# Feature-major projections: both PSUM banks of a block as one tile

## The chip, the cores and the metric

The kernel runs on one core of one Trainium2 chip. The metric is the device time of one execution in microseconds (us), taken as the median of three runs. A core has five engines that run their own instruction streams in order and meet through semaphores: PE (matrix multiply, with PEld, its weight loads), DVE (vector), ACT (scalar), POOL, and SP, which issues most of the DMAs. Matmul results land in PSUM, 128 partitions by 8 banks of 2 KB; everything else that the engines work on lies in SBUF.

## The reference

One layer of an encoder trunk on 256 tokens of width 2048, all in float32. Only the sizes matter here:

```python
h = rms_norm(x, norm_mix_g)
proj = h @ w_in                       # 2048 -> 18464, split in ten parts
rq, rk = rope(...)                    # retention: 8 heads, chunks of 64
q, k, v = silu(causal_conv(gqkv))     # gated delta rule: 16 heads of 128
x = x + (sigmoid(ga) * yr + sigmoid(gb) * yg) @ w_out
q = rms_norm(x) @ w_q ; k, v = split(rms_norm(mem) @ w_kv)
x = x + (softmax(q k^T) v) @ w_o      # 4 heads of 512, 256 memory tokens
x = x + square(relu(rms_norm(x) @ w_ff1)) @ w_ff2    # hidden 8192
return rms_norm(x)
```

## The kernel before, in words

**Products in three parts.** Each float32 operand is split in a rounded high part and the rest (`hi` by an ACT copy, `lo` by a DVE subtraction, lines 125 and 126 for weights). A product is hi·hi + hi·lo + lo·hi. Weights come from HBM in pieces of 1 MB (`raw`, three buffers), and each piece is split in two steps of 128x1024 elements into `whi` and `wlo` (three buffers each; in the last stage every fourth piece uses a single further pair `whx`, `wlx`).

**Feature-major blocks.** `blocks_in_steps` computes 256 output features for 256 tokens: the weights are the stationary operand, the activations the moving one. A block has two groups of 128 features, b = 0 and 1, one PSUM bank each (`s0` and `s1`). Line 210 issues for each of 16 steps of the contraction and each b one matmul of 512 columns (`whi` against hi and lo side by side) and one of 256 columns (`wlo` against hi), so 64 matmuls in a block. At the end, for each b apart, ACT copies the second half of the bank to a tile `bo` (line 219), DVE adds the first half (line 220), and a function of the caller, `evac(b, o)`, goes on with 128x256 elements. There are 96 blocks: 8 for the keys of the memory, 24 for the delta rule's q, k, v, 8 for retention's q, k, 8 in each of two residual projections (`residual_pass`), 8 for the cross-attention's q and 32 for `w_ff1`.

**Token-major products** (`chunk`, lines 166 to 168, and the second MLP product, line 1227 in `with_seven`) use the same PSUM tiles through `stream_ps()`, for tokens 0 to 127 and 128 to 255. In `with_seven` the finished bank is added to the result by line 1142 (`res = bank * r + res`, 128x512 on DVE); `own[n][t]` is the bank of column group n and token half t, `read((n, t, bank))` notes that it is to be added, and the next product puts the addition ahead of its own matmuls.

**What sets the order.** A scheduler places each engine's instructions from the program text, priorities (`tc.high_priority`) and its own forecast of times; `tc.issue_after` fixes some pairs. Then the engines run these fixed orders. A tile of a pool is given out again when its last readers are done: `s0`, `s1` have two buffers each, so a block uses the banks of the block before the last. In three of four parts of the MLP (`early`) the order of blocks and products on PE is fixed by `ends`; in the first part and in the residual passes the scheduler may mix the matmuls of neighbouring blocks.

Beside these, `residual_pass` sums squares in `acc2` and closes with four matmuls of `acc2` against ones (line 1042); `evac_h` makes the squared ReLU of the MLP's hidden layer (lines 1432 to 1438).

Of the kernel before, what the change touches and what calls it, by code (L numbers as in the profile page):

```python
# [17 lines left out]
P = 128  # L18
# [34 lines left out]
def trunk(ctx: ExitStack, tc: tile.TileContext, x_f, mem_f, positions, lead_f, small_f, w_in, ret_gn_g, w_out, w_xq,  # L53
# [12 lines left out]

    def stream_ps():
        s0 = psp.tile([P, 512], F32, name="s0", tag="s0", bufs=2)
        s1 = psp.tile([P, 512], F32, name="s1", tag="s1", bufs=2)
        return s0, s1  # L70
# [121 lines left out]
    def blocks_in_steps(quads, w, c0, nb, evac, ends=None, even=False):  # L192

        k = 16 // nb
        ps = stream_ps()
        n = nb * P
        for g in range(KT // k):  # L200
            halves = fetch([(0, w[g * k * P:(g + 1) * k * P, c0:c0 + n])], k, n, at=AT_BLOCKS)
            for h in range(2):
                these = [(i, b, part) for i in range(k // 2) for b in range(nb) for part in range(2)]
                if even and g == h == 0:
                    these.sort(key=lambda a: a[2])
                for i, b, part in these:
                    kk = (2 * g + h) * k // 2 + i
                    x = quads[kk // 4][0] if part else quads[kk // 4].both
                    with tc.issue_after(ends[-1]) if ends else ExitStack():
                        ins = pe.matmul(ps[b][:, :S] if part else ps[b], halves[h][part][:, i, b * P:(b + 1) * P],  # L210
                                        x[:, kk % 4, :], start=kk == 0 and not part, stop=kk == KT - 1 and part == 1).ins
                if ends is not None:
                    ends.append(ins)
                step()
                yield
        for b in range(nb):
            with tc.high_priority(offset=50000):
                o = sm.tile([P, S], F32, name="bo", tag="bo", bufs=2)
                act.activation(o, ps[b][:, S:], AF.Copy)  # L219
                vec.tensor_add(o, o, ps[b][:, :S])  # L220
                evac(b, o)
# [5 lines left out]
    def narrow(quads, w, c0, n, evac):  # L227
# [12 lines left out]
        with tc.high_priority(offset=50000):  # L240
            o = sm.tile([P, S], F32, name="bo", tag="bo", bufs=2)[:n]
# [382 lines left out]
    for b2 in range(8):  # L624
        ko = kv.tile([P, 2, S], F32, name="ko", tag="vo", bufs=2)

        def evac_k(b, ps):
            vec.tensor_mul(ko[:, b, :], ps, mrow)
# [35 lines left out]
    def gdn_stream(grp):  # L664
# [3 lines left out]
        for pr in range(2):  # L668
# [5 lines left out]
            for part, c0, bofs in ((1, C_GQ, 0), (0, C_GK, 16), (2, C_GV, 32)):  # L674
                def evac(b, ps, part=part, bofs=bofs):
                    if part < 2:
                        conv_silu(bofs + h0 + b, ps, kq[:, b, part, :])
                    else:
                        vt = mx.tile([P, S], F32, name="vt", tag="vt", bufs=2)
                        conv_silu(bofs + h0 + b, ps, vt)  # L680
                        vts.append(vt)
                blocks(h1, w_in[0], c0 + h0 * GD, 2, evac)
# [6 lines left out]
            for b in range(2):  # L689
# [12 lines left out]
                for t, src in enumerate((g0v[:, 0, 0:P], g1v[:, 0, :])):  # L702
                    dj = sm.tile([P, S], F32, name="dj", tag="bo", bufs=2)[:, :P]
# [162 lines left out]
    def retention(j, yr):  # L866
        qk = mx.tile([P, 4, S], F32, name="qk", tag="qk", bufs=1)

        for a2, c0 in ((0, C_RQ), (2, C_RK)):
            def evac_qk(b, ps):  # L870

                rb = mx.tile([P, S], F32, name="rb", tag="rb", bufs=2)
                act.activation(rb[0:64], ps[64:128], AF.Copy)
                act.activation(rb[64:128], ps[0:64], AF.Copy)
                o = qk[:, a2 + b, :]
                vec.tensor_mul(o, ps, cos)
                vec.tensor_mul(rb, rb, sin)
# [131 lines left out]
    def residual_pass(quads, w, gain, name, loader=None, between=None):  # L1009
        nxt = []  # L1010
        acc = xa.tile([P, S], F32, name="acc2", tag="acc2", bufs=2)
        vec.memset(acc, 0.0)
        first_two, held = [], []
        for b2 in range(8):
# [4 lines left out]
            def evac(b, ps, b2=b2, xc=xc):  # L1019
                k = 2 * b2 + b  # L1020
                vec.tensor_add(rt[:, k, :], ps, xc[:, b, :] if loader else rt[:, k, :])
                g = gains[:, gain + k:gain + k + 1]
                qh, ql = (a[:, k % 4, :] for a in nxt[-1])
                act.activation(qh, rt[:, k, :], AF.Copy, scale=g)
                vec.scalar_tensor_tensor(ql, rt[:, k, :], g, qh.bitcast(F32), op0=ALU.mult, op1=ALU.subtract)
                sq = xa.tile([P, S], F32, name="sq2", tag="sq2", bufs=2)
                act.activation(sq, rt[:, k, :], AF.Square)
# [13 lines left out]
        for t in range(NT):  # L1041
            pe.matmul(ps[:, 2 * t:2 * t + 2], acc[:, t * P:(t + 1) * P], ones[:, :2], start=True, stop=True)
# [17 lines left out]
    for h in range(XH):  # L1060
# [10 lines left out]
        for b2 in range(2):  # L1071
            blocks(h2, w_xq[0], h * XD + b2 * 256, 2, lambda b, ps: split(qt, ps, 2 * b2 + b))
# [346 lines left out]
    for fb in range(4):  # L1419
# [5 lines left out]
        for b2 in range(8):  # L1425
# [65 lines left out]
```

## Time and profile before

| what | value |
|---|---|
| three runs | 2044.32, 2045.71, 2046.57 us; median 2045.71 |
| span of the profiled execution, first to last instruction | 2043.3 us |
| PE busy | 2030.5 us (99%), 10802 matmuls |
| PEld busy | 1751.4 us (86%) |
| DVE busy | 1550.6 us (76%) |
| ACT busy | 1184.3 us (58%) |
| the block matmuls of line 210, 512 and 256 columns with `whi`, `wlo` | 969.0 and 765.0 us |
| lines 219 and 220, 192 each | 73.2 and 79.9 us |
| DMA queue q1, share of 16 engines | 62.2% |

Busy time counts an instruction from its start to its end, and matmuls overlap each other. The mean of one 512-column matmul is 390 ns, while the next one starts some 0.23 us after it; the distance of starts is what the stream costs.

### The profile page before, as it was taken

To read this page: it belongs to the slowest core of one execution; us is meant where nothing else is said; L and a number is where in the kernel's file an instruction comes from. 1 tells how busy PE (TensorE), PEld (TensorE's weight loads), DVE (VectorE), ACT (ScalarE), POOL (GpSimd) and SP (SyncE) were. 2 spreads that over 40 slices of the span, in tenths; PEclk is the share of its full clock that TensorE was granted. 3 is DMA by queue.
4 is the path that set the end of the run, shared out by engine and by line. 5 is a ranking of instruction groups with operands and counts; after the bars stand their busy time and mean duration, and the time that the engine had idled before them with its cause. 6 is when DMAs were issued, how large, how long until landed. Compare 5 with 4: busy or idle time off the path is not lost.

```text
span 2043.3 us, 28453 instructions
## 1 busy us (share of the span) xinstructions
PE 2030.5 (99%) x10802; PEld 1751.4 (86%) x10802; DVE 1550.6 (76%) x2423; ACT 1184.3 (58%) x1941; POOL 38.7 (2%) x50
## 2 busy tenths in 40 slices
PE   9999999999999999999999999999999999999998
PEld 7888888988888888888888899888888888888886
DVE  5887788779667875888567666777867887888788
ACT  6655764575457554755446565555547656656655
POOL 0000000000000000000000000000000000000000
PEclk9999999999999999999999999999999999999999
DMA  9689556466555655555467655569657656665761
GB/s 329 209 259 303 184 185 197 154 189 201 180 166 183 198 190 165 186 181 190 156 212 244 191 183 163 174 180 254 221 168 234 219 163 214 201 204 166 242 231 62
DMA packets 329370, 405.24 MB, mean 198 GB/s; under 512 B 34944, under 2 KB 239632, under 8 KB 329104
## 3 DMA queue, kind: packets, MB, share of 16 engines
q1 hardware_dynamic: 328800, 402.74, 62.2%
q8 instruction: 84, 1.38, 0.3%
q10 hardware_dynamic: 432, 0.69, 0.1%
q14 instruction: 54, 0.44, 0.1%
HBM read 389.74 MB, written 11.55 MB: 196 GB/s over the span
## 4 chain that ended last, share of the span: by engine, by line
PE 97%; DVE 2%; issue 0%; DMA 0%; ACT 0%; SPq 0%; DVEq 0%; POOLq 0%; POOL 0%; ACTq 0%
PE s L210 52%; PE s L167 8%; PE s L168 8%; PE s L166 8%; PE b L1227 7%; PE s L1227 7%; PE s L400 1%; PE s L401 1%; PE s L402 1%; PE b L795 1%; PE b L698 1%; PE b L138 1%; PE b L828 1%; PE b L137 1%; PE b L139 1%
## 5 line engine op out<-in xcount | busy, mean ns | idle before, releaser
L210 PE MATMUL s<-q,whi 128*128 128x512 f32 x2816 | 969.0, 390 | 0.6 <-DVE bo L220 0.6
L126 DVE TENSOR_TENSOR wlo<-raw,whi 128x1024 fp32r<-128x1024 f32 x586 | 715.1, 1222 | 296.3 <-ACT whi L125 291.7
L125 ACT ACTIVATE whi<-raw 128x1024 fp32r<-128x1024 f32 x586 | 620.8, 1060 | 488.9 <-PE s L210 209.2
L210 PE MATMUL s<-q,wlo 128*128 128x256 f32 x2816 | 765.0, 281 | 0.0
L210 PEld LDWEIGHTS s<-q,whi 128*128 128x128 f32 x2816 | 520.6, 188 | 101.4 <-DVE bo L220 0.9
L210 PEld LDWEIGHTS s<-q,wlo 128*128 128x128 f32 x2816 | 527.2, 188 | 12.6 <-DVE wlo L126 0.5
L167 PE MATMUL s<-wlo,q 128*128 128x512 f32 x704 | 277.2, 394 | 0.0
L168 PE MATMUL s<-whi,q 128*128 128x512 f32 x704 | 274.9, 391 | 0.0
L166 PE MATMUL s<-whi,q 128*128 128x512 f32 x704 | 254.4, 391 | 0.0
L166 PEld LDWEIGHTS s<-whi,q 128*128 128x128 f32 x704 | 132.1, 188 | 27.4
L168 PEld LDWEIGHTS s<-whi,q 128*128 128x128 f32 x704 | 132.3, 188 | 26.2
L167 PEld LDWEIGHTS s<-wlo,q 128*128 128x128 f32 x704 | 132.3, 188 | 26.2
L219 ACT ACTIVATE bo<-s 128x256 f32<-128x256 f32 x192 | 73.2, 381 | 105.5 <-PE s L210 105.5
L220 DVE TENSOR_TENSOR bo<-bo,s 128x256 f32<-128x256 f32 x192 | 79.9, 416 | 43.0 <-ACT bo L219 42.8
L1227 PE MATMUL s<-whi,q 128*128 128x512 f32 x280 | 90.4, 389 | 0.0
L1250 DVE TENSOR_TENSOR wlo<-rt,whi 128x1024 fp32r<-128x1024 f32 x54 | 65.8, 1224 | 32.3 <-ACT whi L1249 31.6
L210 PE MATMUL s<-q,whx 128*128 128x512 f32 x256 | 89.2, 389 | 0.0
L125 ACT ACTIVATE whx<-raw 128x1024 fp32r<-128x1024 f32 x58 | 61.5, 1060 | 43.2 <-PE b L1227 17.2
L126 DVE TENSOR_TENSOR wlx<-raw,whx 128x1024 fp32r<-128x1024 f32 x58 | 70.9, 1222 | 17.9 <-ACT whx L125 17.4
L1249 ACT ACTIVATE whi<-rt 128x1024 fp32r<-128x1024 f32 x54 | 57.2, 1060 | 38.1 <-PE s L1227 17.8
L210 PE MATMUL s<-q,wlx 128*128 128x256 f32 x256 | 70.4, 280 | 0.0
L1227 PE MATMUL b<-whi,q 128*128 128x512 f32 x216 | 70.3, 389 | 0.0
(350 smaller groups left out, 2372.2 us busy)
## 6 DMA issues: line engine op xcount, KB each, us to landing
raw<-w_in SPq DMA_DIRECT2D x143, 1024.0 KB
raw<-w_ff SPq DMA_DIRECT2D x100, 1024.0 KB
raw<-w_xkv SPq DMA_DIRECT2D x29, 1024.0 KB
raw<-w_out SPq DMA_DIRECT2D x16, 1024.0 KB
raw<-w_xq SPq DMA_DIRECT2D x16, 1024.0 KB
raw<-w_xo SPq DMA_DIRECT2D x16, 1024.0 KB
rt<-w_ff SPq DMA_DIRECT2D x14, 1024.0 KB
tr<-w_ff SPq DMA_DIRECT2D x14, 1024.0 KB
```

Of the source, the lines that this page charges most:

```text
L125: latest["hi"] = act.activation(hi[:, cs], src[:, cs], AF.Copy).ins
L126: latest["lo"] = vec.tensor_sub(lo[:, cs], src[:, cs], hi[:, cs].bitcast(F32)).ins
L137: pe.matmul(o, lhs[0], rhs[0], start=first, stop=False)
L166: pe.matmul(o, xh, wh, start=first, stop=False)
L167: pe.matmul(o, xh, wl, start=False, stop=False)
L168: pe.matmul(o, xl, wh, start=False, stop=last)
L210: ins = pe.matmul(ps[b][:, :S] if part else ps[b], halves[h][part][:, i, b * P:(b + 1) * P], x[:, kk % 4, :], start=kk == 0 and not part, ...
L219: act.activation(o, ps[b][:, S:], AF.Copy)
L220: vec.tensor_add(o, o, ps[b][:, :S])
L1227: ins = pe.matmul(o, lhs[l], rhs[r], start=key not in opened, stop=last and j == 2, skip_group_check=True).ins
L1249: latest["hi"] = act.activation(hi, raw[:, c:c + 1024], AF.Copy).ins
L1250: latest["lo"] = vec.tensor_sub(lo, raw[:, c:c + 1024], hi.bitcast(F32)).ins
```

## The change

Both banks of a block become one PSUM tile `s` of 128x2x512 with two buffers; `stream_ps` hands out its halves. ACT copies 128x2x256 elements with one instruction, DVE adds with one, and each `evac` gets both feature groups at once: 96 copies and 96 additions of 512 elements stand where 192 of 256 stood, and most of what follows (the keys' scaling, the rotation, the residual addition and its squares, the split of q, the squared ReLU) is done for both at once too. The causal convolution and the scaling by the norm's gains stay one instruction for each group. `acc2`, `sq2` and `rb` become 128x2x256 with one buffer instead of two of 128x256; `bo` becomes twice as large with two buffers. `acc2` now holds two groups, so the closing sum has eight matmuls instead of four. The space for `bo` is taken from a reserved area, `dynamic_dma_scratch_size=8192`: in the built programs it goes from 16384 to 8192 bytes of a partition, weights and the tiles behind them move down by 8192 bytes, and the tiles behind `bo` by 6144. No matmul of lines 166 to 168, 210 and 1227 is added, removed or resized.

```diff
+    def stream_both():
+        return psp.tile([P, 2, 512], F32, name="s", tag="s", bufs=2)
+
     def stream_ps():
-        s0 = psp.tile([P, 512], F32, name="s0", tag="s0", bufs=2)
-        s1 = psp.tile([P, 512], F32, name="s1", tag="s1", bufs=2)
-        return s0, s1
+        both = stream_both()
+        return both[:, 0, :], both[:, 1, :]
...
-        ps = stream_ps()
+        both = stream_both()
+        ps = both[:, 0, :], both[:, 1, :]
...
-        for b in range(nb):
-            with tc.high_priority(offset=50000):
-                o = sm.tile([P, S], F32, name="bo", tag="bo", bufs=2)
-                act.activation(o, ps[b][:, S:], AF.Copy)
-                vec.tensor_add(o, o, ps[b][:, :S])
-                evac(b, o)
+        with tc.high_priority(offset=50000):
+            o = sm.tile([P, 2, S], F32, name="bo", tag="bo", bufs=2)
+            act.activation(o, both[:, :, S:], AF.Copy)
+            vec.tensor_add(o, o, both[:, :, :S])
+            evac(o)
...
-            def evac(b, ps, b2=b2, xc=xc):
-                k = 2 * b2 + b
-                vec.tensor_add(rt[:, k, :], ps, xc[:, b, :] if loader else rt[:, k, :])
...
+            def evac(ps, b2=b2, xc=xc):
+                got = rt[:, 2 * b2:2 * b2 + 2, :]
+                vec.tensor_add(got, ps, xc if loader else got)
+                for k in range(2 * b2, 2 * b2 + 2):
...
+                sq = xa.tile([P, 2, S], F32, name="sq2", tag="sq2", bufs=1)
+                act.activation(sq, got, AF.Square)
                 vec.tensor_add(acc, acc, sq)
...
-            pe.matmul(ps[:, 2 * t:2 * t + 2], acc[:, t * P:(t + 1) * P], ones[:, :2], start=True, stop=True)
+            for b in range(2):
+                pe.matmul(ps[:, 2 * t:2 * t + 2], acc[:, b, t * P:(t + 1) * P], ones[:, :2], start=b == 0, stop=b == 1)
...
-            def evac_h(b, ps):
+            def evac_h(ps):
                 if early:
                     act.activation(ps, ps, AF.Relu)
-                    act.activation(hs[:, b, :], ps, AF.Square)
+                    act.activation(hs, ps, AF.Square)
                 else:
-                    vec.scalar_tensor_tensor(hs[:, b, :], ps, 0.0, ps, op0=ALU.max, op1=ALU.mult)
-                qh, ql = (a[:, b2 % 2 * 2 + b, :] for a in hid[-1])
-                act.activation(qh, hs[:, b, :], AF.Copy)
-                vec.tensor_sub(ql, hs[:, b, :], qh.bitcast(F32))
-                if b2 < 4 and b:
+                    vec.scalar_tensor_tensor(hs, ps, 0.0, ps, op0=ALU.max, op1=ALU.mult)
+                split(hid[-1], hs, slice(b2 % 2 * 2, b2 % 2 * 2 + 2))
+                if b2 < 4:
                     token_sums(b2, hs)
...
-    nc = bacc.Bacc("TRN2", target_bir_lowering=False, num_devices=1)
+    nc = bacc.Bacc("TRN2", target_bir_lowering=False, num_devices=1, dynamic_dma_scratch_size=8192)
```

How the orders move is shown at three places. Rows of the change bear the changed kernel's line numbers (213 for 210, 222 for 220, 1232 for 1227, 1147 for 1142); the numbers behind names tell buffers apart, and a bracket names the engines or DMA queues whose semaphores the instruction waits for.

**Place A, PE, the second MLP product, once in each of the three `early` parts:** the end of the product into `own[0][0]` and the start of the one into `own[0][1]`. Before:

```order
L1227 MATMUL s0_15391<-whi_15491,q_14671 128x512 [waits Activation_49]
L1227 MATMUL s0_15391<-wlo_15492,q_14671 128x512 [waits DVE_49]
L1227 MATMUL s0_15391<-whi_15491,q_14671 128x512 x2
L1227 MATMUL s0_15391<-wlo_15492,q_14671 128x512
L1227 MATMUL s0_15391<-whi_15491,q_14671 128x512
L1227 MATMUL s1_15392<-whi_15507,q_14454 128x512 [waits Activation_49]
L1227 MATMUL s1_15392<-wlo_15508,q_14454 128x512 [waits DVE_49]
```

The same place in the change, first on PE and then on DVE:

```order
L1232 MATMUL s_14856<-whi_14954,q_14184 128x512 [waits Activation_49]
L1232 MATMUL s_14856<-wlo_14955,q_14184 128x512 [waits DVE_49]
L1232 MATMUL s_14856<-whi_14954,q_14184 128x512 x2
L1232 MATMUL s_14856<-wlo_14955,q_14184 128x512
L1232 MATMUL s_14856<-whi_14954,q_14184 128x512
L1232 MATMUL s_14856<-whi_14970,q_13983 128x512 [waits DVE_49,Activation_49]
L1232 MATMUL s_14856<-wlo_14971,q_13983 128x512
```

```order
L1255 TENSOR_TENSOR wlo_14971<-rt_9911,whi_14970 128x1024 [waits Activation_49]
L1255 TENSOR_TENSOR wlx_14975<-rt_9911,whx_14974 128x1024 [waits Activation_49]
L128 TENSOR_TENSOR wlo_14994<-raw_14991,whi_14993 128x1024 [waits DMAHW4_49,Activation_49]
L1147 SCALAR_TENSOR_TENSOR res_12593<-s_14856,rstd3q_12587,res_12593 128x512 [waits PE_49]
L128 TENSOR_TENSOR wlo_14998<-raw_14991,whi_14997 128x1024 [waits Activation_49]
```

The two banks are one tile `s_14856` now, and the first matmul into its second bank waits for DVE, where the next matmul, which needs the split `wlo_14971`, waits for nothing more. The DVE count that it waits for is reached by the addition of line 1147 that reads the first bank of the tile. On DVE this addition stands behind the splits of the same product and one split for the next one.

**Place B, PE and DVE, the first residual projection:** `s_9924` is block 0, `s_10022` block 1, `s_10121` block 2, which uses block 0's banks again; before, these are the pairs from `s0_10165`, `s0_10271` and `s0_10378`. PE before, the end of block 0, and 42 rows further on the start of block 2:

```order
L210 MATMUL s1_10166<-q_9832,wlo_10216 128x256
L210 MATMUL s0_10271<-q_10051,whi_10279 128x512 [waits Activation_49]
L210 MATMUL s0_10271<-q_10051,wlo_10280 128x256 [waits DVE_49]
L210 MATMUL s1_10272<-q_10051,whi_10279 128x512
L210 MATMUL s1_10272<-q_10051,wlo_10280 128x256
```

```order
L210 MATMUL s1_10272<-q_9832,whi_10321 128x512
L210 MATMUL s1_10272<-q_9832,wlo_10322 128x256
L210 MATMUL s0_10378<-q_10014,whi_10382 128x512 [waits Activation_49]
L210 MATMUL s1_10379<-q_10014,whi_10382 128x512 [waits DVE_49,PE_49]
L210 MATMUL s0_10378<-q_10014,wlo_10383 128x256 [waits DVE_49]
```

In the change, PE at the end of block 0, PE at the start of block 2, and DVE:

```order
L213 MATMUL s_9924<-q_9593,wlo_9974 128x256
L213 MATMUL s_10022<-q_9847,wlo_10068 128x256
L213 MATMUL s_10022<-q_9593,whi_10071 128x512 [waits Activation_49]
L213 MATMUL s_10022<-q_9593,wlo_10072 128x256 [waits DVE_49]
L213 MATMUL s_10022<-q_9593,whi_10071 128x512
```

```order
L213 MATMUL s_10022<-q_9593,whi_10071 128x512
L213 MATMUL s_10022<-q_9593,wlo_10072 128x256
L213 MATMUL s_10121<-q_9773,whi_10124 128x512 [waits DVE_49]
L213 MATMUL s_10121<-q_9773,wlo_10125 128x256
L213 MATMUL s_10121<-q_9773,whi_10124 128x512
```

```order
L136 TENSOR_TENSOR ktl_10725<-kr_10720,kth_10724 128x1024 [waits DMAHW6_49,Activation_49]
L128 TENSOR_TENSOR wlo_10125<-raw_10122,whi_10124 128x1024 [waits DMAHW2_49,PE_49]
L1075 SCALAR_TENSOR_TENSOR vvl_10727<-vr_10722,nm_r_773,vvh_10726 128x512 [waits DMAHW7_49,Activation_49]
L1075 SCALAR_TENSOR_TENSOR vvl_10727<-vr_10722,nm_r_773,vvh_10726 128x512 [waits Activation_49]
L128 TENSOR_TENSOR wlo_10129<-raw_10122,whi_10128 128x1024 [waits DVE_49,PE_49,Activation_49]
L222 TENSOR_TENSOR bo_10009<-bo_10009,s_9924 128x512 [waits Activation_49]
```

Before, 48 matmuls of block 1 stood between the end of block 0 and the start of block 2; now there are 17. Block 2 waits for the last of these DVE rows, the addition that frees block 0's banks (line 222). The first wait for PE in them, at `wlo_10125`, is for the last matmul of block 0, the first row of the change's PE rows.

**Place C, PE, the start of `w_ff1`:** `s_12604` is block 0, `s_12707` block 1; before, these are `s0_13017` and `s0_13127`, and `s0_13238` is block 2. Before, the end of block 0, and 11 rows further on the first use of `whx` in block 1:

```order
L210 MATMUL s1_13018<-q_12784,whx_13067 128x512
L210 MATMUL s1_13018<-q_12784,wlx_13068 128x256
L210 MATMUL s0_13238<-q_12127,whi_13242 128x512 [waits DVE_49]
L210 MATMUL s0_13238<-q_12127,wlo_13243 128x256
L210 MATMUL s0_13238<-q_12127,whi_13242 128x512
```

```order
L210 MATMUL s0_13238<-q_12366,whi_13246 128x512
L210 MATMUL s0_13238<-q_12366,wlo_13247 128x256
L210 MATMUL s0_13127<-q_12784,whx_13177 128x512 [waits Activation_49]
L210 MATMUL s1_13128<-q_12784,whx_13177 128x512
L210 MATMUL s0_13127<-q_12784,wlx_13178 128x256 [waits DVE_49]
```

In the change:

```order
L213 MATMUL s_12604<-q_12385,whx_12653 128x512
L213 MATMUL s_12604<-q_12385,wlx_12654 128x256
L213 MATMUL s_12707<-q_12385,whx_12756 128x512 [waits Activation_49]
L213 MATMUL s_12707<-q_12385,wlx_12757 128x256 [waits DVE_49]
L213 MATMUL s_12707<-q_12385,whx_12756 128x512
```

`whx` and `wlx` have one buffer each. Between the last use of the old contents of `whx` and the first use of the new ones stood 17 matmuls; now there is one, the 256-column matmul of `wlx_12654`. The wait for DVE ahead of block 2, which stood right behind block 0, now stands 16 matmuls behind it.

More of the change, by code (lines that the diff above doesn't have):

```diff
@@ L674, in gdn_stream, with evac @@
             for part, c0, bofs in ((1, C_GQ, 0), (0, C_GK, 16), (2, C_GV, 32)):
[L675 to L681, printed above, removed]
+                def evac(o, part=part, bofs=bofs):
+                    for b in range(2):
+                        if part < 2:
+                            conv_silu(bofs + h0 + b, o[:, b, :], kq[:, b, part, :])
+                        else:
+                            vt = mx.tile([P, S], F32, name="vt", tag="vt", bufs=2)
+                            conv_silu(bofs + h0 + b, o[:, b, :], vt)
+                            vts.append(vt)
                 blocks(h1, w_in[0], c0 + h0 * GD, 2, evac)
@@ L1010, in residual_pass @@
         nxt = []
-        acc = xa.tile([P, S], F32, name="acc2", tag="acc2", bufs=2)
+        acc = xa.tile([P, 2, S], F32, name="acc2", tag="acc2", bufs=1)
         vec.memset(acc, 0.0)
@@ L1071, in trunk @@
         for b2 in range(2):
-            blocks(h2, w_xq[0], h * XD + b2 * 256, 2, lambda b, ps: split(qt, ps, 2 * b2 + b))
+            blocks(h2, w_xq[0], h * XD + b2 * 256, 2, lambda o: split(qt, o, slice(2 * b2, 2 * b2 + 2)))
         sps = bank()
```

29 lines of the change are left out of this document (14 added, 15 removed).

## The prediction

> **What bounds the kernel now.** I read the first page, then who waited on PE, then the timeline around PE's one long pause. The page's busy shares and chain:
>
> ```profile
> PE 2030.5 (99%) x10802; PEld 1751.4 (86%) x10802; DVE 1550.6 (76%) x2423; ACT 1184.3 (58%) x1941; POOL 38.7 (2%) x50
> PE 97%; DVE 2%; issue 0%; DMA 0%; ACT 0%; SPq 0%; DVEq 0%; POOLq 0%; POOL 0%; ACTq 0%
> ```
>
> PE is busy for all but 13 us, and the chain that ended last runs through it for 97%. A busy PE may still hide waits, so the waits of PE alone, complete:
>
> ```profile
> PE b L258 <- DVE warm L254: 1.1, 1, 1.1
> PE s L400 <- ACT q L348: 0.8, 1, 0.8
> PE s L210 <- DVE bo L220: 0.6, 1, 0.6
> PE s L400 <- DVE q L335: 0.3, 1, 0.3
> ```
>
> Three of the four are start-up. Between start-up and the end only one wait is listed, 0.6 us. So work taken off ACT or DVE has almost nothing to give back, while whatever newly makes PE wait adds its full length: PE has no slack to catch up in. The question is which waits of PE are new.
>
> This is PE's one listed pause at work, in the timeline (start, duration, idle before in brackets), and what it costs:
>
> ```profile
> 1367.93 0.28 PE L210 MATMUL s<-q,wlx 128*128 128x256 f32 x1
> 1368.31 0.42 DVE L220 TENSOR_TENSOR bo<-bo,s 128x256 f32<-128x256 f32 x1 [1.37 <-ACT bo L219]
> 1368.79 0.19 PEld L210 LDWEIGHTS s<-q,whi 128*128 128x128 f32 x1 [0.90 <-DVE bo L220]
> 1368.79 0.50 PE L210 MATMUL s<-q,whi 128*128 128x512 f32 x1 [0.58 <-DVE bo L220]
> 1369.13 0.28 PE L210 MATMUL s<-q,wlo 128*128 128x256 f32 x1
> 1369.24 0.39 PE L210 MATMUL s<-q,whi 128*128 128x512 f32 x1
> 1369.47 0.28 PE L210 MATMUL s<-q,wlo 128*128 128x256 f32 x1
> ```
>
> In the stream a 512-column matmul is followed after 0.23 us (1369.24 to 1369.47), a 256-column one after 0.12 (1369.13 to 1369.24); a pair takes 0.345. Here 0.86 passes after the 256-column one, 0.74 too much. PE goes on 0.06 after DVE's end (1368.31 + 0.42 = 1368.73), and the first distance afterwards is 0.34 instead of 0.23, since the weight load starts only with the matmul: 0.11 more. I use both for every pause. [...]
>
> **The change part by part.**
>
> The larger operations. The rows of what is replaced, and of the nearest operations with 512 elements:
>
> ```profile
> L219 ACT ACTIVATE bo<-s 128x256 f32<-128x256 f32 x192 | 73.2, 381 | 105.5 <-PE s L210 105.5
> L220 DVE TENSOR_TENSOR bo<-bo,s 128x256 f32<-128x256 f32 x192 | 79.9, 416 | 43.0 <-ACT bo L219 42.8
> L133 ACT ACTIVATE q<-b 128x512 fp32r<-128x512 f32 x10 | 5.8, 590 | 6.9 <-PE b L139 5.8 <-PE b L277 1.1
> L693 DVE TENSOR_TENSOR kl<-kq,kh 128x512 fp32r<-128x512 f32 x16 | 11.0, 685 | 0.0
> ```
>
> 96 copies at 0.59 are 56.6 us against 73.2 on ACT, 96 additions at 0.685 are 65.8 against 79.9 on DVE; the later steps save in proportion. All of it lies beside PE and is worth 0 on the path. The cover is the other pair of banks: most blocks (11 us, 32 pairs) have a whole block between their end and the next use of their banks, against 0.59 + 0.69 for the copy and the addition. Where that cover is gone is place B.
>
> Place A, three times. PE may write `own[0][1]` only when DVE has read `own[0][0]`, its neighbour in the tile. Before, these are the rows (1638.14 stands for two matmuls, the second at 1638.37, the first one into `own[0][1]`):
>
> ```profile
> 1638.14 0.62 PE L1227 MATMUL s<-whi,q 128*128 128x512 f32 x2
> 1638.31 1.23 DVE L126 TENSOR_TENSOR wlo<-raw,whi 128x1024 fp32r<-128x1024 f32 x1
> 1639.45 0.74 DVE L1142 SCALAR_TENSOR_TENSOR res<-s,rstd3q,res 128x512 f32<-128x512 f32 x1
> 1808.26 0.62 PE L1227 MATMUL s<-whi,q 128*128 128x512 f32 x2
> 1809.56 0.74 DVE L1142 SCALAR_TENSOR_TENSOR res<-s,rstd3q,res 128x512 f32<-128x512 f32 x1
> 1978.39 0.61 PE L1227 MATMUL s<-whi,q 128*128 128x512 f32 x2
> 1979.69 0.74 DVE L1142 SCALAR_TENSOR_TENSOR res<-s,rstd3q,res 128x512 f32<-128x512 f32 x1
> ```
>
> The addition ends at 1639.45 + 0.74 = 1640.19, PE would go on at 1640.25 instead of 1638.37: 1.88 us. The order on DVE is the same in the change, the split of L126 first. The other two give 1.87 each. With 0.11 each this is 3 x 1.99 = **+6.0**. Were the split out of the way, the addition would start 0.04 after the bank's last matmul, and the pause would still be 0.39 + 0.04 + 0.74 + 0.06 - 0.23 = 1.0: bounds 3.3 to 6.0. Behind PE's wait stands the whole rest of the product; ACT and DVE wait for PE's weights buffers and shift with it.
>
> Place B. DVE rows before at the same place, a pair of splits showing how two in a row overlap:
>
> ```profile
> 1071.81 1.23 DVE L134 TENSOR_TENSOR ktl<-kr,kth 128x1024 fp32r<-128x1024 f32 x1 [1.63 <-ACT kth L133]
> 1073.61 0.75 DVE L1070 SCALAR_TENSOR_TENSOR vvl<-vr,nm_r,vvh 128x512 fp32r<-128x512 f32 x1 [0.25 <-ACT vvh L1069]
> 1077.81 2.36 DVE L126 TENSOR_TENSOR wlo<-raw,whi 128x1024 fp32r<-128x1024 f32 x2
> ```
>
> From the start of block 0's last matmul: 0.28 for it, 0.04 to DVE, then split, `vvl` twice, split, addition: 1.23 + 2 x 0.75 + 1.23 + 0.69 = 4.65, less four overlaps of 0.09, so 4.3; 0.06 back to PE: 4.7. PE covers 2 x 0.12 + 8 x 0.345 = 3.0. Pause 1.7, with 0.11 1.8. If the `ktl` split is still running when block 0 ends it is 2.9 at most. I take **+2.0**, nearer the row without it, since the block ends later in the new order. Another block of this kind, with 16 matmuls of cover in the second residual pass, has one split and the addition behind it: 0 to 0.5, taken as 0.
>
> Place C. The copy into `whx` and the split into `wlx`:
>
> ```profile
> 1368.18 1.05 ACT L125 ACTIVATE whx<-raw 128x1024 fp32r<-128x1024 f32 x1
> 1369.26 1.22 DVE L126 TENSOR_TENSOR wlx<-raw,whx 128x1024 fp32r<-128x1024 f32 x1
> ```
>
> From the start of the last use of the old `whx`: 0.39 + 0.04 + 1.05 + 0.06 = 1.54; PE is there at 0.35, a pause of 1.19. Its next matmul needs `wlx`, at 1.48 + 0.04 + 1.22 + 0.06 = 2.80, and is due at 1.77: 1.03, and 0.11 at the end: **+2.3**. Bounds 0, if other matmuls came between, and 2.3. The old pause there goes, 0.74 + 0.11: **-0.85**; the addition that it waited for now has 16 matmuls, 2.8 us, of cover.
>
> The closing sums. Four rows before take 0.36 us:
>
> ```profile
> 1357.48 0.50 PE L1042 MATMUL b<-ones,acc 128*128 128x2 f32 x4
> 1357.84 0.47 PE L210 MATMUL s<-q,whi 128*128 128x512 f32 x1
> ```
>
> Four more at each of two places: **+0.7**. The end after PE's last matmul consists of additions and scalings that the change leaves alone: 0. The shift of the tiles moves no row that I can see; 0, bounds in the rivals.
>
> Sum: 6.0 + 2.0 + 2.3 - 0.85 + 0.7 = +10.2. The span goes from 2043.3 to 2053.5. The median of the runs lies 2.4 above the span (2045.71), so the forecast is **2055.9 us**, 0.5% slower.
>
> **The rivals.**
>
> A alone: B and C hang on what stands where between neighbouring blocks, and DVE or ACT may be further ahead there than the rows say. Then 2045.71 + 6.0 - 0.85 + 0.7 = 2051.6. For it: before, 48 and 17 matmuls hid the same work. Against it: the fixed DVE order of B and the single `whx` buffer leave no way around.
>
> Waits by bank: DVE reads bank 0 of the tile while PE writes bank 1, and a wait only for its own bank would cost A nothing. B, C and the sums stay: 2045.71 + 2.0 + 2.3 - 0.85 + 0.7 = 2049.9. Against it stands the order of the change, which lists the wait. [...]
>
> Not slower: the stream itself gets faster, from the moved tiles or from less traffic of ACT and DVE. Its place is line 210, 3072 pairs. The price of one nanosecond a pair is 3.1 us, so it decides from 10.2 / 3.07 = 3.3 ns of a pair's 345. The nearest rows on how far operands change the stream:
>
> ```profile
> L210 PE MATMUL s<-q,whi 128*128 128x512 f32 x2816 | 969.0, 390 | 0.6 <-DVE bo L220 0.6
> L167 PE MATMUL s<-wlo,q 128*128 128x512 f32 x704 | 277.2, 394 | 0.0
> L1227 PE MATMUL s<-whi,q 128*128 128x512 f32 x280 | 90.4, 389 | 0.0
> ```
>
> They differ by 5 ns between quite different tiles, so 3.3 is possible but large; the shifts here are multiples of 2048 bytes. A gain of that size gives 2045.7, one of 5 ns 2040.5. The same shift may cost instead: 2 ns a pair give 2062.
>
> **How the numbers follow.** Forecast (A, B and C) 0.65; A alone 0.15; waits by bank 0.04; a slower stream 0.06; a faster one 0.10, of which half ends within 0.2% (4.1 us, what a measurement of this kernel can tell from no change) and half below. The range from 2049.5 to 2060 holds the first three and the bounds of B (2.9) and of the other block; left out are 0.16. Slower 0.90, same 0.05, faster 0.05.
>
> **What would show it.** In the waits of PE: three waits of about 1.9 of line 1232 for DVE's `res`, one near 1.7 for `bo` in the first residual projection, one each for `whx` and `wlx` at the start of `w_ff1`, and no wait right behind block 0 there. Pairs of line 213 should stay at 0.345, and DVE and ACT lose some 30 us of busy time or more without a gain. Wrong would be: pauses of A that are absent or near 1.0 (the split is not ahead), B or C absent, or a changed distance in the stream.

## The result, and the profile after

The changed kernel took 2062.02 us (median of four runs, 2060.64 to 2062.99), the kernel before 2046.14 beside it (2044.32 to 2047.34): a ratio of 1.0079, 95% interval 1.0067 to 1.0092. That is 15.9 us slower. The forecast was 10.2 us slower, 2055.9, with a range up to 2060: the sign was right, the time lies 2 us above the range.

The first page of the change, with the busy times and the chain that ended last:

```profile
PE 2037.0 (99%) x10810; PEld 1756.2 (85%) x10810; DVE 1528.6 (74%) x2215; ACT 1161.4 (56%) x1725; POOL 36.0 (2%) x50
PE 96%; DVE 1%; DMA 1%; ACT 1%; issue 0%; SPq 0%; DVEq 0%; POOLq 0%; POOL 0%; ACTq 0%
```

ACT and DVE are busy for 23 and 22 us less, and the kernel is slower: what they do lies beside PE. The waits of PE (in total, times, longest) name the places:

```profile
PE s L1232 <- DVE res L1147: 5.4, 3, 1.8
PE s L213 <- DVE bo L222: 2.7, 1, 2.7
PE b L260 <- DVE warm L256: 1.1, 1, 1.1
PE s L213 <- ACT whx L127: 1.0, 1, 1.0
PE s L213 <- DVE wlx L128: 0.8, 1, 0.8
PE s L402 <- DVE q L337: 0.5, 1, 0.5
PE s L169 <- DVE wlo L128: 0.3, 1, 0.3
```

Three of 1.8 us at A, one of 2.7 at B, two at C, and the old wait of 0.6 for `bo` behind block 0 of `w_ff1` is gone: all six forecast waits are there, on the forecast lines. They add up to 9.9 us of idle time. The rest is in no list of waits. It shows in the timeline of PE behind the third pause of A (start, duration):

```profile
1992.35 0.47 PE L1232 MATMUL s<-whi,q 128*128 128x512 f32 x1 [1.81 <-DVE res L1147]
1992.65 0.40 PE L1232 MATMUL s<-wlo,q 128*128 128x512 f32 x1
...
1993.36 0.63 PE L1232 MATMUL s<-wlo,q 128*128 128x512 f32 x1
1993.79 0.63 PE L1232 MATMUL s<-whi,q 128*128 128x512 f32 x1
1994.21 0.63 PE L1232 MATMUL s<-whx,q 128*128 128x512 f32 x1
...
1996.35 0.59 PE L1232 MATMUL s<-whx,q 128*128 128x512 f32 x1
1996.77 0.39 PE L1232 MATMUL s<-whi,q 128*128 128x512 f32 x1
1997.00 0.39 PE L1232 MATMUL s<-wlo,q 128*128 128x512 f32 x1
```

From 1993.36 to 1996.77 a 512-column matmul follows after 0.43 us where the stream has 0.23, although PE is busy all the time. The table by stretches shows it too. A row gives the stretch and its length, the busy time (and number of instructions) of PE, PEld, DVE, ACT and POOL, the granted clock of PE as a share of its full one, the busy share of the DMA engines and GB/s:

```profile
1989.90:1993.30 3.40, 1.59 (x7) 1.03 (x6) 3.26 (x5) 2.16 (x4) 0.00 (x0) 1.00 0.50 145
1993.30:1996.70 3.40, 3.40 (x9) 2.66 (x9) 1.75 (x3) 1.06 (x1) 0.00 (x0) 0.51 0.98 342
1996.70:2000.10 3.40, 3.40 (x16) 2.75 (x15) 2.09 (x3) 2.05 (x4) 0.00 (x0) 0.99 0.35 134
```

After the pause PE ran at half clock (0.51) for 3.4 us and did 9 matmuls instead of 16, which costs another 1.6 us. The same follows the two pauses of C:

```profile
1373.00:1375.60 2.60, 0.84 (x4) 0.22 (x2) 1.24 (x2) 1.54 (x2) 0.00 (x0) 0.99 1.05 316
1375.60:1379.00 3.40, 3.36 (x11) 2.90 (x12) 1.39 (x2) 1.06 (x1) 0.00 (x0) 0.51 1.19 228
```

The distances between the starts of PE's matmuls, less the usual 0.228 and 0.118, give what each place costs. The last matmul starts 15.6 us later than before:

| place | forecast | measured |
|---|---|---|
| A, three pauses: 1.97 each, 0.08 at the next matmul | 6.0 | 6.15 |
| B: 2.82 and 0.11 | 2.0 | 2.93 |
| C: 1.19, 1.03 and 0.11 | 2.3 | 2.33 |
| old pause behind block 0 of `w_ff1` | -0.85 | -0.85 |
| second residual projection: 0.30 and 0.11 | 0 | 0.41 |
| eight closing matmuls more | 0.7 | 0.9 |
| half clock behind C and behind the third pause of A | 0 | 3.1 |
| first 12 us | 0 | 1.25 |
| remainder | | -0.6 |

The first 12 us are no part of the change: matmuls run at double distance there (0.43 us from one of 512 columns to the next, 0.23 afterwards) until 10.0 us. In the profiles of the experiments, whose work there is the same, this ends anywhere between 3.6 and 10.2 us, and the first 12 us take between 0.4 us less and 1.4 more than in the profile of before.

### The profile page after: what moved, and what is told of

Same layout as the page of the kernel before. It is cut to its first block, busy times and chain, and to the rows that moved or that the text cites. A ratio compares the mean times of both kernels' runs of the same rounds, so it can differ in the third digit from the quotient of the medians.

```text
span 2058.9 us, 28031 instructions
## 1 busy us (share of the span) xinstructions
PE 2037.0 (99%) x10810; PEld 1756.2 (85%) x10810; DVE 1528.6 (74%) x2215; ACT 1161.4 (56%) x1725; POOL 36.0 (2%) x50
## 4 chain that ended last, share of the span: by engine, by line
PE 96%; DVE 1%; DMA 1%; ACT 1%; issue 0%; SPq 0%; DVEq 0%; POOLq 0%; POOL 0%; ACTq 0%
PE s L213 51%; PE b L1232 8%; PE s L169 8%; PE s L168 7%; PE s L170 7%; PE s L1232 7%; PE s L402 1%; PE s L404 1%; PE s L403 1%; PE b L798 1%; DVE wlo L128 1%; PE b L701 1%; PE b L140 1%; PE b L831 1%; PE b L139 1%; PE b L141 1%
## 5 line engine op out<-in xcount | busy, mean ns | idle before, releaser
L213 PE MATMUL s<-q,wlo 128*128 128x256 f32 x2816 | 785.6, 281 | 0.0
L213 PEld LDWEIGHTS s<-q,whi 128*128 128x128 f32 x2816 | 527.6, 188 | 112.8 <-DVE bo L222 3.4
L168 PE MATMUL s<-whi,q 128*128 128x512 f32 x704 | 275.4, 391 | 0.0
L170 PE MATMUL s<-whi,q 128*128 128x512 f32 x704 | 274.6, 390 | 0.0
L168 PEld LDWEIGHTS s<-whi,q 128*128 128x128 f32 x704 | 132.2, 188 | 27.0
L170 PEld LDWEIGHTS s<-whi,q 128*128 128x128 f32 x704 | 132.3, 188 | 26.6
L1232 PE MATMUL s<-whi,q 128*128 128x512 f32 x280 | 91.5, 391 | 5.4 <-DVE res L1147 5.4
L1232 PEld LDWEIGHTS s<-whi,q 128*128 128x128 f32 x280 | 52.8, 189 | 17.5 <-ACT whi L127 6.6
L222 DVE TENSOR_TENSOR bo<-bo,s 128x512 f32<-128x512 f32 x96 | 65.3, 680 | 0.0
```

The lines of the kernel that those rows point to most:

```text
L168: pe.matmul(o, xh, wh, start=first, stop=False)
L170: pe.matmul(o, xl, wh, start=False, stop=last)
L222: vec.tensor_add(o, o, both[:, :, :S])
L1232: ins = pe.matmul(o, lhs[l], rhs[r], start=key not in opened, stop=last and j == 2, skip_group_check=True).ins
```

## The experiments

Theory 1 is that of the table: the pauses of A, B and C, and a half clock that some of them bring. The rivals were a stream that is slower everywhere (from the layout or otherwise), waits that do not come from the tile, and a lighter ACT and DVE that are worth something after all. Times are medians, beside runs of the kernel before on the same chip.

**Layout alone.**

```diff
-    nc = bacc.Bacc("TRN2", target_bir_lowering=False, num_devices=1)
+    nc = bacc.Bacc("TRN2", target_bir_lowering=False, num_devices=1, dynamic_dma_scratch_size=8192)
```

> The kernel before with the reserved area of 8192 bytes of the change and nothing else: weights and the tiles behind them lie 8192 bytes lower, the order of every engine is that of before. Theory 1: 2045.5, no change. Rival, the moved tiles make the stream slower (by 2 ns a pair) or faster: 2051.6 or 2039.

Measured: 2045.78 against 2045.42, ratio 1.0001 (0.9992 to 1.0009). Moving the tiles does nothing; the rival of a faster or slower stream, to which the prediction gave 0.16, falls as far as it hangs on the reserved area.

**The joint tile alone**, in the kernel before:

```diff
-        s0 = psp.tile([P, 512], F32, name="s0", tag="s0", bufs=2)
-        s1 = psp.tile([P, 512], F32, name="s1", tag="s1", bufs=2)
-        return s0, s1
+        both = psp.tile([P, 2, 512], F32, name="s", tag="s", bufs=2)
+        return both[:, 0, :], both[:, 1, :]
```

> The kernel before with one part of the change alone: the two banks of a block are one tile; all operations stay apart for each feature group, acc2 and the layout stay. Theory 1, the joint tile alone makes the pauses and the larger operations do not: place A costs 6.2 us as in the change and 1.6 for each half-clock stretch behind it, and the blocks whose banks are used again soon wait for two copies and two additions (0.38 + 0.42 us each) of both groups instead of one of each: 2060 or more, the order of PE showing waits at the starts of both residual projections and of w_ff1. Rival, B and C come from the larger operations (acc2, the order that they bring): 2045.5 + 6.2 + 1.6 = 2053.3, without waits of the block matmuls for bo above 1 us.

Measured: 2075.17 against 2045.42, ratio 1.0145 (1.0131 to 1.0158): 29.7 us slower, nearly twice the whole change. Its waits of PE:

```profile
PE s L209 <- DVE bo L219: 6.7, 2, 4.0
PE s L1226 <- DVE res L1141: 5.4, 3, 1.8
PE s L209 <- DVE wlx L125: 2.6, 2, 2.2
PE b L136 <- ACT pth L132: 1.1, 1, 1.1
...
PE s L209 <- ACT whx L124: 0.9, 1, 0.9
PE b L137 <- DVE ptl L133: 0.9, 1, 0.9
```

A is the same as in the change, as nothing else of the change has a part in it. The wait for `bo` is 4.0 us long where the change has 2.7: block 2 needs both halves of its tile free, and with separate operations two copies and two additions stand ahead of that. In this trace the second addition ends 1.8 us after the first (1082.39 and 1084.19), with a split and a residual addition between them on DVE. Half clock lasts 23.9 us in all between the start and PE's last matmul (granted clock 0.50), 6.8 us in the change. So the joint tile alone costs 30 us, and the whole change is about 14 us faster than that. How much of the 14 the larger operations give isn't separated: the scheduler's orders differ too, and the 17.1 us more of half clock cost up to half of their length, 8.5 us by estimate. The rival, 2053.3, falls.

**Place A undone.** `own[0][0]` is read after both products:

```diff
             product(own[0][0], part(1, 0), b21, (0, 0))
-            read((0, 0, own[0][0], True))
             product(own[0][1], part(1, 1), b11, (0, 1))
-            read((0, 1, own[0][1], True))
+            read((0, 0, own[0][0], True), (0, 1, own[0][1], True))
```

> The changed kernel (2062.0 us), but in the MLP's early parts the product into own[0][1] follows the one into own[0][0] directly and both additions come after it, so PE does not wait there. Theory 1, the time is lost in the three pauses of place A, in those of B and C, and in stretches of 3.4 us at half clock that follow some pauses (granted clock 0.51 after C and after the third pause of A in the profile of the change): 3 x 2.08 = 6.2 us of pauses go, and with them the half-clock stretch behind the third one, 1.7: 2054 to 2056. In the profile no wait of line 1232 for DVE and no half-clock stretch in the second MLP products. Rival, only the pauses count and the rest is a stream that is slower everywhere: 2055.8, and distances in the stream above those of before outside the pauses. Rival, the tile is not what makes PE wait: 2062.

Measured: 2053.15 (ratio 1.004, 1.0027 to 1.0052), 8.9 less than the change. No wait of line 1232 is left and no half clock in the second products; 8.9 is 6.15 for the pauses and 2.7 more, 0.85 beyond the expected bound. That could be half clock behind more than one of the three pauses in the runs without a profile, or the start, whose time differs by up to 1.8 us between profiles; which of them isn't shown. B, C and the half clock behind C stay.

**Place C undone.** Block 1's last piece goes to `whi` and `wlo`; the list `skip` holds the number of that piece:

```diff
-        if spare and turn[0] % 4 == 0:
+        if spare and turn[0] % 4 == 0 and turn[0] not in skip:
...
+            if (fb, b2) == (0, 1):
+                skip.append(turn[0] + 4)
```

> The changed kernel, but at the start of w_ff1 the last piece of block 1 goes to the three-buffered whi and wlo, not to the single whx and wlx. Theory 1: both pauses of place C (1.19 and 1.03 us and 0.1) go, and the half-clock stretch of 3.4 us behind them, 1.7 us: 2062.0 - 2.3 - 1.7 = 2058.0. Rival, the half clock there is not a consequence of the pauses: 2059.7, with granted clock 0.51 still there at that place.

Measured: 2057.32 (ratio 1.006, 1.0047 to 1.0073), 4.7 less than the change where 4.0 were expected. Both waits are gone, and so is the half clock at that place; it is a consequence of the pauses.

**Place B, DVE's order.** The splits of keys and values come later:

```diff
-        split(kt, kr)
-        for t in range(NT):
+        with tc.issue_after(latest["lo"]):
+            split(kt, kr)
+            for t in range(NT):
```

> The changed kernel, but the splits of the first cross-attention head's keys and values (ktl, vvl) are issued after the residual projection's last weights, so that the addition that frees block 0's banks has one split ahead of it on DVE, not four operations. Theory 1: the pause at place B, 2.8 + 0.1 us in the profile of the change, shrinks to 0.5 or less: 2062.0 - 2.4 = 2059.6. Rival, the pause comes from the order of PE (17 matmuls between the end of block 0 and the start of block 2) and would be there with any DVE order: 2061.5 to 2062.

Measured: 2058.83 (ratio 1.0069, 1.0056 to 1.0081), 3.2 less. By the time theory 1 would do, but the profile says otherwise: the wait for `bo` is 1.6 us, and the pause 1.77 instead of the 0.5 expected, so only 1.05 us of it went. The rest of the 3.2 lies within what half-clock stretches change from run to run (2057.1 to 2062.1 here, with four of them in the profiled run). In this trace the splits of keys and values are gone from DVE's chain, but ACT still makes their copies (`kth` and `vvh`, 1076.30 to 1078.98) ahead of the copy of the next weights, for which DVE idles 1.29 us, and block 0's own copy to `bo` starts only at 1079.83. So the edit took the work from one of two engines, and this run doesn't decide for the rival, the order of PE.

**A, B (late splits) and C together.**

> The changed kernel with all three of these edits (products into own[0] together, ktl and vvl late, whi for whx in block 1). Theory 1: 2062.0 - 6.2 - 2.4 - 2.3 - 3.4 = 2047.7; what is left over before (2046.1) is the four more closing matmuls at two places (0.7), the small pause of the second residual projection (0.4) and of the first (0.5) and perhaps 1 us in the first 10 us, less the old pause of 0.85. Rival, a stream that is slower everywhere by 4 us: 2051. Rival, the lighter ACT and DVE are worth something once the pauses are gone: below 2045.

Measured: 2047.82 (ratio 1.0011, 1.0002 to 1.002), the expected 2047.7. That it agrees to 0.1 us is luck, since the pause at B is still 1.66 us where the sum had 0.5. Between the start and PE's last matmul no half clock is left in its profile, and the waits of PE hold one line from the change:

```profile
PE s L213 <- DVE bo L222: 1.5, 1, 1.5
```

**A, C and PE's order at B.** `lead` holds block 0's last matmul, and the second half of block 1 comes after it; the splits of keys and values stay where they were in the program text:

```diff
-                    with tc.issue_after(ends[-1]) if ends else ExitStack():
+                    with tc.issue_after(ends[-1]) if ends else tc.issue_after(lead[0]) if lead and g else ExitStack():
...
+        if lead is not None and not lead:
+            lead.append(ins)
```

> The changed kernel with the edits of place A (additions after both products) and C (whi for whx), and at place B an edit of PE's order alone: the second half of block 1 of the first residual projection comes after block 0's last matmul, so that 33 matmuls stand between the end of block 0 and block 2 instead of 17; DVE's order is left to the scheduler. Theory 1: 33 matmuls cover the 4.7 to 5.9 us chain on DVE, no pause is left at B, and the 1.8 us go that the version with late ktl and vvl (2047.8) still had there: 2046.0, the time of before (2045.6). Rival, the pause at B moves to the weights or to the last part of the merged activations that block 0 needs: 2047.5 or more, with a new wait there.

Measured: 2045.82 against 2045.40, ratio 1.0002 (0.9993 to 1.0011). All the waits of PE above 0.1 us:

```profile
PE b L262 <- DVE warm L258: 1.1, 1, 1.1
PE s L169 <- DVE wlo L128: 0.9, 1, 0.9
PE s L404 <- DVE q L339: 0.6, 1, 0.6
```

The wait for `bo` is gone. But PE's order isn't all that moved. These are ACT's copy and DVE's addition of block 0 in this version:

```profile
1076.76 0.58 ACT L223 ACTIVATE bo<-s 128x512 f32<-128x512 f32 x1
1076.89 1.23 DVE L128 TENSOR_TENSOR wlo<-raw,whi 128x1024 fp32r<-128x1024 f32 x1 [1.55 <-ACT whi L127]
1078.03 0.68 DVE L224 TENSOR_TENSOR bo<-bo,s 128x512 f32<-128x512 f32 x1
1078.63 1.22 DVE L136 TENSOR_TENSOR ktl<-kr,kth 128x1024 fp32r<-128x1024 f32 x1
```

The scheduler has put the addition ahead of `ktl` and `vvl`. It ends 3.1 us after the start of block 0's last matmul (1075.60 to 1078.71), where it took 5.8 in the change (1077.70 to 1083.47). For such a chain the 3.0 us of 17 matmuls would nearly do, so the run shows that the wait goes with the new orders of both engines, and not that 33 matmuls cover the chain of the change. With A, B and C out of the way, the changed kernel is as fast as before: the whole 16 us are these places and what follows from them.

**The closing sums.** On top of that, `acc2` is 128x256 again:

```diff
-                vec.tensor_add(acc, acc, sq)
+                for b in range(2):
+                    vec.tensor_add(acc, acc, sq[:, b, :])
...
-            for b in range(2):
-                pe.matmul(ps[:, 2 * t:2 * t + 2], acc[:, b, t * P:(t + 1) * P], ones[:, :2], start=b == 0, stop=b == 1)
+            pe.matmul(ps[:, 2 * t:2 * t + 2], acc[:, t * P:(t + 1) * P], ones[:, :2], start=True, stop=True)
```

> The version without the pauses of A, B and C (2045.8) with the closing sums as before: acc2 is 128x256 again and takes two additions of 256, so that four matmuls close it instead of eight, twice: 0.7 us less, 2045.1 against 2045.4 of the kernel before. Rival, the lighter ACT and DVE are worth something that the doubled sums hid: below 2044.

Measured: 2045.10 against 2045.42, ratio 0.9997 (0.9988 to 1.0006): 0.7 below the version with eight, which is within the intervals of the two, and not to be told from the kernel before. ACT and DVE are 24 and 21 us less busy than before in it, and that is worth nothing.

**How long must a pause be to bring half clock?** Three versions in which only place A is left of the pauses, in three lengths. As in the change:

> The same with place A as in the change: 2046.0 + 3 x 2.08 = 2052.2 and 1.6 us for each half-clock stretch behind one of the three pauses. So far 5 of 9 such pauses (idle 1.9 us each) had one: 0 to 3 stretches, 2052.2 to 2057.0, most runs near 2054.5, and run to run more spread than in the version without pauses.

Measured: 2052.52 (2051.67 to 2052.59), ratio 1.0032 (1.0019 to 1.0044): the three pauses and hardly more than that, 6.7 above the version without them. The profiled run has one half-clock stretch. The spread was expected wider.

Shorter, with the next splits behind the addition (`freed` holds the addition, and the splits of the next piece are issued after it):

```diff
-                    latest["lo"] = vec.tensor_sub(lo[:, cs], src[:, cs], hi[:, cs].bitcast(F32)).ins
+                    with tc.issue_after(freed[0]) if freed else ExitStack():
+                        latest["lo"] = vec.tensor_sub(lo[:, cs], src[:, cs], hi[:, cs].bitcast(F32)).ins
```

> As a_only, but DVE splits the next weights after the addition: the three pauses are 1.0 us instead of 1.97. Three pauses of 1.1: 2046.0 + 3.3 = 2049.3. Theory 1: an idle time of 0.8 us or so is too short for the half clock, so 2049.3. Rival, any pause can bring it: up to 2054.

Measured: 2049.59 (ratio 1.0021, 1.0012 to 1.003). The pauses:

```profile
PE s L1237 <- DVE res L1152: 2.8, 3, 0.9
...
PE s L215 <- DVE wlo L129: 1.0, 2, 0.5
```

Three of 0.9 us idle, 1.10 lost each, and no half clock behind any in the profiled run. The runs reach from 2048.32 to 2052.80, and only one of them has a profile, so half clock in the slower ones isn't excluded. The second row is a loss that the edit brought and that was not expected: two pauses of 0.7 at the start of `w_ff1`, behind a split.

Longer, with two more operations on the bank:

```diff
         with tc.issue_after(latest["lo"]):
             add(n, t, ps)
+            if longer:
...
+                    for _ in range(2):
+                        vec.scalar_tensor_tensor(got, ps, 0.0, got, op0=ALU.mult, op1=ALU.add)
```

> As a_only, but two more DVE operations that read own[0][0] (adding it times zero) stand behind the addition, with the second split between them: the three pauses are 4.3 us. Theory 1: 2046.0 + 3 x 4.4 = 2059.2, and the half clock follows every time, since PE is idle for more than a whole stretch of 3.4 us: 3 x 1.6 more, 2064.0, with three stretches of granted clock 0.51 in the profile. Rival, the half clock has nothing to do with the length of the pause: 2059.2 to 2061.

Measured: 2066.73 (ratio 1.01, 1.0084 to 1.0115), above the 2064.0 of theory 1 and far above the rival's 2059 to 2061. Its waits, and the stretch around the first pause:

```profile
PE s L1243 <- DVE res L1164: 12.8, 3, 4.3
```

```profile
1637.00:1640.00 3.00, 2.96 (x14) 2.10 (x12) 1.50 (x2) 2.13 (x3) 0.00 (x0) 1.00 0.59 229
1640.00:1644.00 4.00, 0.00 (x0) 0.00 (x0) 3.97 (x5) 1.05 (x1) 0.00 (x0) 0.74 0.87 259
1644.00:1648.70 4.70, 4.48 (x11) 3.54 (x12) 0.53 (x2) 1.06 (x1) 0.00 (x0) 0.50 0.65 226
1648.70:1652.00 3.30, 3.30 (x16) 2.74 (x15) 2.65 (x3) 1.06 (x1) 0.00 (x0) 0.99 0.00 0
```

The clock is halved while PE still waits (0.74 on the average of those 4 us), and stays so for 4.4 to 5.7 us after it: behind all three pauses, and more than the one stretch of 3.4 us expected. Each pause costs (2066.73 - 2045.82) / 3 = 7.0 us, 4.5 of it the pause.

## Why the prediction was right or wrong

**The bound and the method** held. PE had no slack (99% busy), what newly made it wait cost its whole length (6.15 us for the 5.4 of waits at A), and what became lighter beside it gave nothing: 2045.10 with all the larger operations but the addition into `acc2`, and none of the pauses. The busy time taken off ACT and DVE was 23 and 22 us, together more than the 16.6 and 14.1 that the prediction's rows gave for the copies and additions alone.

**Place A** was right in its size (6.0, measured 6.15) and its cause. The timeline of the change has the order that was argued, split first and then the addition:

```profile
1646.02 0.39 PE L1232 MATMUL s<-whi,q 128*128 128x512 f32 x1
...
1646.18 1.23 DVE L128 TENSOR_TENSOR wlo<-raw,whi 128x1024 fp32r<-128x1024 f32 x1
...
1647.32 0.75 DVE L1147 SCALAR_TENSOR_TENSOR res<-s,rstd3q,res 128x512 f32<-128x512 f32 x1
...
1648.18 0.19 PEld L1232 LDWEIGHTS s<-whi,q 128*128 128x128 f32 x1 [2.20 <-ACT whi L127]
1648.21 0.47 PE L1232 MATMUL s<-whi,q 128*128 128x512 f32 x1 [1.81 <-DVE res L1147]
```

The lower bound, 1.0 with the split out of the way, was measured too: 1.10. The rival of waits by bank falls with the wait itself (three of 1.8 us) and with its going when the two products no longer have the addition between them (no wait of line 1232 is left). The weight load that starts only with the matmul cost 0.08 here instead of 0.11: the load starts 0.03 us before the matmul (1648.18 and 1648.21).

**Place B** is the first step that failed, as a size: 2.0 was taken, 2.93 measured, and the upper bound was 2.9. The bound was for the case that the `ktl` split is still running when block 0 ends, and that is what happened:

```profile
1076.96 1.06 ACT L135 ACTIVATE kth<-kr 128x1024 fp32r<-128x1024 f32 x1 [0.66 <-DMA kr<-kt_d]
...
1077.70 0.40 PE L213 MATMUL s<-q,wlo 128*128 128x256 f32 x2
...
1078.05 1.22 DVE L136 TENSOR_TENSOR ktl<-kr,kth 128x1024 fp32r<-128x1024 f32 x1 [3.26 <-ACT kth L135]
...
1079.19 1.22 DVE L128 TENSOR_TENSOR wlo<-raw,whi 128x1024 fp32r<-128x1024 f32 x1
...
1080.33 1.41 DVE L1075 SCALAR_TENSOR_TENSOR vvl<-vr,nm_r,vvh 128x512 fp32r<-128x512 f32 x2
...
1081.65 1.22 DVE L128 TENSOR_TENSOR wlo<-raw,whi 128x1024 fp32r<-128x1024 f32 x1
...
1082.79 0.68 DVE L222 TENSOR_TENSOR bo<-bo,s 128x512 f32<-128x512 f32 x1
...
1083.52 0.50 PE L213 MATMUL s<-q,whi 128*128 128x512 f32 x1 [2.67 <-DVE bo L222]
```

DVE idled 3.26 us for the `kth` copy, which had waited for a transfer, and so `ktl` ended at 1079.27 and the split behind it started at 1079.19, 1.2 after block 0 would have let it (1077.70 + 0.28 + 0.04 = 1078.02). The prediction chose the other case "since the block ends later in the new order". That argument compared PE's order with DVE's times of before and forgot that the transfer of `kr`, which starts the chain, could move as well. It did: block 0's last matmul starts 6.4 us later (1071.26 before, 1077.70 in the change), the transfer is issued 4.2 us later (1065.9 and 1070.1), and `ktl` starts 6.2 us later (1071.81 and 1078.05). So the two kept their distance to 0.2 us, and in the rows of before `ktl` already starts only when block 0 has ended. Among rows in one fixed order on an engine, what an operation ahead waits for is part of the sum.

**The other block of this kind**, taken as 0 within 0 to 0.5, cost 0.41.

**Place C and the old pause** were right: 2.33 and -0.85. **The closing sums** cost 0.9 instead of 0.7: eight matmuls take 0.81 us at each of the two places (here from 1362.87 on, to the start of the next row), where the four before took 0.36.

```profile
1362.87 0.95 PE L1047 MATMUL b<-ones,acc 128*128 128x2 f32 x8
1363.67 0.47 PE L213 MATMUL s<-q,whi 128*128 128x512 f32 x1
```

**What was not in the sum at all** is the half clock, and that is what put the time out of the range. Neither the sum nor a bound nor a rival asked what PE does after a pause; the range ended where the pauses' own bounds ended. The change's median lies 15.9 above before. The pauses and sums make 11.9 (6.15 + 2.93 + 2.33 - 0.85 + 0.41 + 0.9), with which the time would have stayed inside the range. That leaves 4.0, between two and three stretches of 1.6. The step to add is a term of its own for each new pause of a length that was followed by half clock here (1.8 to 4.3 us): half of the usual 3.4 us, times the chance that it follows (7 of 15 at 1.8). That the rival of a stream 2 ns slower a pair gave 2062, the time measured, is chance: outside the half clock the pairs of line 213 stay at 0.345 us, and the moved tiles alone cost nothing.

**The chance** can be read from the runs. The ends of half-clock stretches lie on a grid: 1377.33, 1650.40, 1824.55 and 1998.66 in the run with late splits are 0, 80.00, 131.02 and 182.03 times 3.4133 us apart from the first; 10.02, 1378.98 and 1996.77 in the change 0, 401.07 and 582.06 times. The steps in the trace's own record of the granted clock lie on the same grid: in the change they stand at 10.20, 1375.53, 1378.95, 1993.34, 1996.76 and 2051.37 us, 0, 400, 401, 581, 582 and 598 times 3.4133 us from the first, with 0.50 granted from 1375.53 to 1378.95 and from 1993.34 to 1996.76. On it, pauses of one length divide by where in a cell, a stretch of 3.41 us from one point of the grid to the next, they begin:

| idle time of PE | pauses | followed by half clock |
|---|---|---|
| 0.9 (shorter A) | 3 | 0 |
| 1.5 to 1.6 (B with late splits) | 2 | 0 |
| 1.8 (A in five runs) | 15 | 7 |
| 1.8 to 2.0 in two parts (C in three runs, the tile alone at 1279) | 4 | 4 |
| 2.5 to 2.7 (B in three runs, the tile alone at 1296) | 4 | 1 |
| 4.0 to 4.3 (longer A, B with the tile alone) | 4 | 4 |

Three pauses close together in the tile alone (1379 to 1388, with 10.2 us of half clock) are left out. Of the 19 pauses in one part with 1.8 to 2.7 us of idle time, the eight with half clock began 0.09 to 0.97 us into a cell, and the eleven without at 1.17 to 3.33. So it matters where a pause begins, and since a cell begins at another place of the program in another run (the record's first step is at 4.37 us before and at 10.20 in the change, 1.71 cells apart), the same pause costs 1.6 us in one run and nothing in the next: the first of A was followed by half clock in the run with late splits (0.53 from 1647.0 to 1650.4) and not in the change (1.00 from 1646 to 1652). To lie inside one cell is not enough: pauses that began at 1.17 to 1.56 did so as well (1.17 + 1.81 = 2.98), and no half clock followed. For shorter pauses the table says little: only one of the three of 0.9 us began early in a cell (at 0.70), and the two of 1.5 to 1.6 began at 3.1 and 3.3. Why C brought half clock three times out of three with as much idle time in two parts isn't settled, and neither is what within a cell decides.

## What to carry to other kernels

When two PSUM banks become one tile, look for each place where one bank is read while the other is written, and for each place where a tile is used again soon: here the wait was for the whole tile, and with PE 99% busy it cost its full length (6.15 us for the three at A, 2.93 at B), and the larger operations did not repay that. A pause on PE can have a second price: of those of 1.8 us, 7 of 15 were followed by 3.4 us at half clock, some 1.6 us each. Orders that keep the tile and avoid the pauses (additions after both products, an earlier end of the block whose banks are used again, a piece in another buffer) brought the kernel back to 2045.1 to 2045.8 us, no faster than before.

## What the runs showed of the hardware

- Idle time of 1.8 us on PE (place A in five runs) was followed by a granted clock of 0.5 for 3.4 us in 7 of 15 pauses, those that began 0.09 to 0.97 us into a cell of the grid; 0.9 us in none of 3 (shorter A); 4.3 us in all 3 (longer A), there for 4.4 to 5.7 us after the pause.
- The ends of such stretches lie on a grid of 3.413 us, over 1987 us of one run (10.02 to 1996.77 in the change).
- At the start matmuls went at double distance (0.43 us for 512 columns instead of 0.23, in the change) until 3.6 to 10.2 us, different from run to run, while the granted clock of the profile reads 1.00 there. The clock's record in these traces begins only at the end of that stretch (at 4.37 us before, at 10.20 in the change), so the distances, not that column, show it.
- Moving all weight tiles by 8192 bytes changed the time by a ratio of 1.0001 (0.9992 to 1.0009).
